# Output chains in halves, a corner turn moved, PSUM sums in W_down and a wider halo product, in a Hymba-style layer on one core

## The chip, the cores and the metric

The kernel runs on one NeuronCore of a Trainium2 chip. The metric is device time in microseconds (us), the median of several runs. TensorE is called PE, VectorE DVE, ScalarE ACT, GpSimd POOL and SyncE SP, as in the profile.

## The reference

One decoder layer, in float32, on 1024 tokens of width 1024 with 16 learned meta tokens in front:

```python
xn = rms_norm(h, mix_pre_g[l])
proj = xn @ w_in[l]                       # z, xbc, dt, q, k, v
y_ssd = ssd_mixer(z, xbc, dt_raw, ...)    # Mamba-2 scan in chunks of 128, gated and normed
y_sb = rms_norm(stick_breaking_attention(q, k, v).reshape(Bsz, L, SB_WIDTH), sb_norm_g[l])
mix = jnp.concatenate([y_ssd, y_sb], axis=-1) @ w_out[l]
h = h + rms_norm(mix, mix_post_g[l])
xn = rms_norm(h, ffn_pre_g[l])
gu = xn @ w_up[l]
g = causal_dwconv(gu[..., :D_FF], ffn_conv_w[l], ffn_conv_b[l])   # 3 taps
f = (jax.nn.gelu(g, approximate=True) * gu[..., D_FF:]) @ w_down[l]
h = h + rms_norm(f, ffn_post_g[l])
```

The attention has 16 heads of 64 and weighs key s for query t by beta[t,s] times the product of (1 - beta[t,j]) over the keys between them, so each block of 128 queries needs a running product along the keys. D_FF is 2816.

## The kernel before

All large products keep float32 accuracy with three float32r products: an operand is split into a high part (a rounding copy on ACT) and a low part (the difference, a subtraction), and high*high, low*high and high*low are summed in PSUM. So for each weight or activation tile there are an ACT copy and a subtraction on DVE or POOL ahead of TensorE. In the names, `yh`/`yl`, `whi`/`wlo`, `dh`/`dl` and `qh`/`ql` are such parts.

The kernel goes through these stages: norm and input projections with the SSD scan; stick-breaking attention over eight pairs of heads, with the projections of the next pair as filling work; the output projection in two halves of W_out (SSD half, attention half) with the residual and the second norm; W_up with the gate, as seven-product (Strassen-Winograd) blocks; W_down the same way. TensorE's order is the program's own from the attention on and again from the sixth row block of the second output half; there DVE, ACT and POOL are in program order too. In the attention and in the first five row blocks of the second output half a planner orders DVE, ACT, POOL and SP by its own costs.

**Attention, and the change's place in it.** For pair p and query block i, `block_weights` makes the scores `z` (L754) into PSUM pairs `zz` (two of them, shared with `tw`), ACT makes the two sigmoids `kp` and `bt` (L755, L756), DVE scans `kp` (L762), POOL multiplies `bt` by it (L764) and makes the edge columns `cb` (L765). `kp` has two buffers, `bt` three. `block_turn` transposes `bt` on TensorE (`tw`, L776) and ACT copies it out (`th`, L778). `block_mix` multiplies by the values (`av`, L791). Blocks run staggered: scores of block i, values of block i-3, filling work, the turn of block i-2. `turn_v` and `turn_edge` turn a pair's values into token order; `turn_edge` copies the edge columns (L419, L420), transposes them (`vtc`, L422), and prepares the meta tokens' queries, keys and values (`meta_q`, `meta_k`, a store to `mvd`). They are the `post` steps of a pair's projections, one per filling slot.

In the last pair the projections are used up, and the SSD half of the output projection fills in: `wout_steps` scales and splits eight tiles of W_out (`woa`, L876, L877), `split_y` splits the SSD output of a row block (L925 on ACT, L926 on POOL), and `ssd_half` runs for each of the eight row blocks two chains `out_steps` of 24 matmuls (`mo`, L936), one per 512 columns; ACT scales each into `ma` (L951) and SP stores it to `mixd`. One chain runs per query block, after the block's turn; three more while the last turns run out. `halo_rows` (L905) does the same product for the two last meta tokens in plain float32, on two output rows only, with the four column blocks of W_out in four groups of 32 array columns; ACT copies the four pieces out of PSUM into `mh` (L910, one buffer) and SP stores them to `halod` (L911). `halo_block` loads the two halves' rows again, scales and adds them on DVE (L1173, L1175), and passes them through the same residual and norm steps `after` as the other rows (L1097 to L1110; `oxn` is the normed row block that `turn_x2` transposes, L1116).

**W_down.** `DOWN` lists seven products, each of eleven steps of 256 rows. `split_step(s + 3)` splits the two operands of a later step (L1581, L1582; three buffers), `w_sum` makes sums of weight tiles on DVE (L1586; L1579 for product 6), `down_mm` runs 12 matmuls for four row blocks (L1652), each product in its own four PSUM banks. `todo` holds the evacuations of a finished product (`evac2`, into SBUF sums `facc`) and the tails, one item per step. The last 14 steps give the second low part to POOL. The last four steps run row block by row block, each followed by its sum (L1663), its square sum on ACT (L1687), the gain (L1688), POOL's power (L1697, L1698), and the closing multiply-add and store (`end_tail`, L1706).

Of the kernel before, what the change touches and what calls it, by code (L numbers as in the profile page):

```python
# [16 lines left out]
P = 128  # L17
# [34 lines left out]
def tile_layer(ctx: ExitStack, tc: tile.TileContext, x, meta, rows, parts,  # L52
# [80 lines left out]
    halod = [dr.tile([2, D], F32, name=f"halod{n}", tag=f"halod{n}") for n in range(2)]  # L133
# [227 lines left out]
    def qkv_steps(p, post):  # L361
# [67 lines left out]
        post += [lambda: turn_v(0), lambda: turn_v(1), turn_edge]  # L429
# [471 lines left out]
    def halo_rows(pool, half, y0, w, acc):  # L901
        for k in range(8):
            for s in range(2):
                for c in range(4):
                    mm(acc[32 * c:32 * c + 2, 0:256], y0[:, k, :], w[k][s][:, 256 * c:256 * c + 256].bitcast(F32),  # L905
                       start=k == 0 and s == 0, stop=k == 7 and s == 1)
        mh = pool.tile([P, 256], F32, tag="ma", name=f"mh{half}", bufs=1)
        for c in range(4):
            rows_ = slice(32 * c, 32 * c + 2)
            nc.scalar.activation(mh[rows_], acc[rows_, 0:256], AF.Copy)  # L910
            nc.sync.dma_start(out=halod[half][:, 256 * c:256 * c + 256], in_=mh[rows_])  # L911
# [7 lines left out]
    def split_y(pool, half, t, tags, yk=None):  # L919
# [6 lines left out]
        nc.gpsimd.tensor_tensor(yl, yk, yh.bitcast(F32), op=ALU.subtract)  # L926
        return yh, yl

    def out_steps(half, t, w, y, evac):
        yh, yl = y  # L930
        for hf in range(2):
            acc = psum_mm(f"mo{half}_{t}_{hf}")
            cs = slice(512 * hf, 512 * hf + 512)
            for k, (wh, wl) in enumerate(w):
                for j, (u, v) in enumerate(((yh, wh), (yl, wh), (yh, wl))):
                    mm(acc, u[:, k, :], v[:, cs], start=(k == 0 and j == 0), stop=(k == 7 and j == 2))  # L936
# [5 lines left out]
    def ssd_half(w, ys):  # L942
        for t in range(1, NT + 1):
            y = ys.pop(0)
            if t < NT - 1:
                ys.append(split_y(wp, 0, t + 2, ("whi", "wlo", WB)))

# [6 lines left out]
            yield from out_steps(0, t, w, y, ev)  # L954
# [19 lines left out]
    for p in range(8):  # L974
        for i in range(NT):
# [8 lines left out]
            run(fill, 1 + (i < FILL[p]))  # L984
            run(block)
# [16 lines left out]
            while len(ys1) < min(2, left[1]):  # L1002
                ys1.append(split_y(wp, 0, len(ys1) + 1, ("whi", "wlo", WB), yk[len(ys1)]))
# [18 lines left out]
    while turn or mix:  # L1022
# [4 lines left out]
        run(first, 1)  # L1027
    edge = edge_turn(7)
    run(first, 1)
# [27 lines left out]
    for _ in first:  # L1057
        run(second, 2)
# [785 lines left out]
```

## Time and profile before

| what | value |
|---|---|
| median of 3 runs | 1757.07 us (1756.71 to 1760.06) |
| the profiled execution | 1754.64 us, of which the span is 1752.8 us |
| mean granted TensorE clock | 0.994 of full speed |
| PE busy | 1711.4 us, 98% of the span |
| DVE, POOL, ACT busy | 1127.2, 890.3, 820.2 us |
| last pair's blocks and output chains | about 831 to 945 us of the span |
| second output half | about 983 to 1096 us |
| W_down | 1531 to 1745 us, the tail to 1752.8 us |

The span runs from the first to the last of the program's instructions. A row of an engine's timeline has the start, the time from there to the end, the engine, the line, the operation, what is written from what, the shapes, the count, and in brackets the engine's idle time before it and what ended it. Operations of one engine overlap at their ends, so what one costs in a row of them is the distance of the starts.

### The profile page before, as it was taken

How to read it: one execution, taken by the hardware profiler on the slowest of the kernel's cores; microseconds unless marked ns; L12 is line 12 of the kernel's file. 1: busy time of each engine (PE TensorE's matmuls, PEld its weight loads, DVE VectorE, ACT ScalarE, POOL GpSimd, SP SyncE). 2: the span in 40 equal slices, each digit the busy share in tenths (PEclk: the TensorE clock that was granted, in tenths of full speed). 3: DMA queues.
4: the chain of work that ended last, by engine and by line, in shares of the span. 5: the costliest groups of instructions: out<-in, count | busy, mean ns of one | idle time of the engine just before them, and what ended most of it. 6: DMA issues, size and time to landing. Idle time of an engine off the chain costs nothing. (4 is left out here: it accounts for less than half of the span.)

```text
span 1752.8 us, 28312 instructions
## 1 busy us (share of the span) xinstructions
PE 1711.4 (98%) x11358; PEld 1505.3 (86%) x11358; DVE 1127.2 (64%) x1225; ACT 820.2 (47%) x1363; POOL 890.3 (51%) x664
## 2 busy tenths in 40 slices
PE   7999999999999999999899989999999999999997
PEld 6999899788999998998678778889998888888885
DVE  5652964875676686668430457676666666757988
ACT  5423653554566566568453344533333333344453
POOL 4323663585566576556451233487776777400015
PEclk9999999999999999999999999999999999999999
DMA  4143343231011110112214543133332222395334
GB/s 161 50 116 93 107 128 105 65 103 38 26 37 37 38 35 27 37 60 74 81 49 145 199 156 132 62 119 98 106 106 91 90 91 90 122 331 185 96 121 162
DMA packets 90655, 173.87 MB, mean 99 GB/s; under 512 B 10694, under 2 KB 35798, under 8 KB 90524
## 3 DMA queue, kind: packets, MB, share of 16 engines
q1 hardware_dynamic: 90524, 172.07, 30.6%
q8 instruction: 89, 1.46, 0.3%
q14 instruction: 42, 0.34, 0.1%
HBM read 122.32 MB, written 49.72 MB: 98 GB/s over the span
## 5 line engine op out<-in xcount | busy, mean ns | idle before, releaser
L764 POOL TENSOR_TENSOR bt<-bt,kp 128x256 f32<-128x256 f32 (+7 forms) x128 | 212.7, 1681 | 180.4 <-DVE kp L762 150.7
L762 DVE TENSOR_TENSOR_SCAN kp<-kp,hold 128x272 f32<-128x272 f32 (+7 forms) x128 | 184.0, 1478 | 26.2 <-ACT kp L755 17.2
L1197 POOL TENSOR_TENSOR wlo<-wr,whi 128x1024 fp32r<-128x1024 f32 x43 | 107.5, 2508 | 38.0 <-ACT whi L1196 38.0
L1652 PE MATMUL dn<-dl,dh 128*128 128x512 f32 x304 | 118.7, 390 | 1.2 <-POOL dl L1582 1.2
L1652 PE MATMUL dn<-dh,dl 128*128 128x512 f32 x304 | 118.6, 390 | 0.1
L1652 PE MATMUL dn<-dh 128*128 128x512 f32 x304 | 118.5, 390 | 0.0
L1697 POOL TENSOR_TENSOR fms<-fms 128x1 f32<-128x1 f32 x8 | 5.6, 694 | 197.9 <-ACT dh L1581 185.8
L755 ACT ACTIVATE kp<-z 128x288 f32<-128x288 f32 (+6 forms) x112 | 82.6, 737 | 47.8 <-PE z L754 22.1
L1581 ACT ACTIVATE dh<-ar 128x512 fp32r<-128x512 f32 x76 | 48.1, 632 | 112.0 <-PE dn L1652 77.4
L1196 ACT ACTIVATE whi<-wr 128x1024 fp32r<-128x1024 f32 x43 | 45.6, 1060 | 114.8 <-PE fX L1254 68.3
L163 PE MATMUL pj_v<-xs,wh_v 128*128 128x400 f32 (+2 forms) x384 | 94.9, 334 | 0.0
L163 PE MATMUL pj_k<-xs,wh_k 128*128 128x400 f32 (+2 forms) x384 | 94.3, 332 | 0.0
L1326 DVE SCALAR_TENSOR_TENSOR ga<-gr,pp,ga 128x1024 f32<-128x1024 f32 x44 | 71.4, 1622 | 34.7 <-ACT ga L1319 33.9
L163 PE MATMUL pj_q<-xs,wh_q 128*128 128x386 f32 (+2 forms) x384 | 93.7, 331 | 0.0
L778 ACT ACTIVATE th<-tw 128x1024 f32<-128x1024 f32 (+2 forms) x96 | 75.7, 818 | 38.0 <-PE tw L776 37.8
L163 PE MATMUL pj_X<-xs,wh_X 128*128 128x400 f32 (+2 forms) x384 | 93.0, 329 | 0.0
L163 PE MATMUL pj_z<-xs,wh_z 128*128 128x386 f32 (+2 forms) x384 | 91.5, 326 | 0.0
L730 DVE CAST qh<-q 128x128 fp32r<-128x128 f32 x64 | 44.1, 690 | 63.9 <-PE z L754 63.6
L776 PE MATMUL tw<-ident,bt 128*128 128x128 f32 x576 | 78.1, 279 | 5.9 <-ACT bt L756 3.0
L1582 DVE TENSOR_TENSOR dl<-ar,dh 128x512 fp32r<-128x512 f32 x76 | 58.4, 768 | 39.1 <-ACT dh L1581 35.9
L756 ACT ACTIVATE bt<-z 128x288 f32<-128x288 f32 (+6 forms) x112 | 82.9, 740 | 0.0
L936 PE MATMUL mo<-woa,yh 128*128 128x512 f32 x256 | 82.4, 396 | 0.0
(556 smaller groups left out, 5532.3 us busy)
## 6 DMA issues: line engine op xcount, KB each, us to landing
wr<-in_w_up SPq DMA_DIRECT2D x44, 512.0 KB, 4.1
fds<-ga SPq DMA_DIRECT2D x44, 256.0 KB, 2.0
b<-in_w_down SPq DMA_DIRECT2D x44, 256.0 KB, 4.7
ar<-fds SPq DMA_DIRECT2D x44, 256.0 KB, 2.6
fda<-ga SPq DMA_DIRECT2D x33, 256.0 KB, 4.5
ar<-fda SPq DMA_DIRECT2D x33, 256.0 KB, 3.0
yk<-yd SPq DMA_DIRECT2D x16, 512.0 KB, 4.5
wor<-in_w_out SPq DMA_DIRECT2D x12, 512.0 KB, 3.9
```

The source lines that it names most:

```text
L163: mm(acc[:ncol, :n - s], a[:, k, :ncol], xs[c0][:, b, k, s:n], start=(k == 0 and j == 0), stop=(k == KB - 1 and j == 2))
L755: nc.scalar.activation(kp[:, :, a:a + w], z[:, :, :w], AF.Sigmoid, scale=-QSCALE)
L756: nc.scalar.activation(bt[:, :, a:a + w], z[:, :, :w], AF.Sigmoid, scale=QSCALE)
L762: nc.vector.tensor_tensor_scan(kp[:, j][:, ::-1], kp[:, j][:, ::-1], hold[:, L - n:L][:, ::-1], 0.0, op0=ALU.mult, op1=ALU.max)
L764: nc.gpsimd.tensor_tensor(bt[:, j, 0:m], bt[:, j, 0:m], kp[:, j, 1:m + 1], op=ALU.mult)
L776: nc.tensor.transpose(tw[:, j, b, :], bt[:, j, c0:c0 + P], ident)
L778: nc.scalar.activation(th[:, :, :nb, :], tw[:, :, :nb, :], AF.Copy)
L936: mm(acc, u[:, k, :], v[:, cs], start=(k == 0 and j == 0), stop=(k == 7 and j == 2))
L1197: nc.gpsimd.tensor_tensor(l, raw, h.bitcast(F32), op=ALU.subtract)
L1326: nc.vector.scalar_tensor_tensor(v, self.g[jj][:, :, i:i + 256], fconv_w[:, j, i:i + 1], v, op0=ALU.mult, op1=ALU.add)
L1582: (nc.gpsimd.tensor_tensor if k and s >= n2 - LATE else sub)(lo[k], raw, hi[k].bitcast(F32), op=ALU.subtract)
L1652: mm(banks[t], u[0][:, c], v[1], start=(p == 0 and i == 0), stop=(p == NPR - 1 and i == 2))
```

## The change

1. `out_steps` has a second stop in the middle of each chain, so `ssd_half` comes in 32 steps of 12 matmuls. In the last pair one step runs between a block's values and its turn, one after the turn; two at each place after the loop; the weights of the other half are spread one to each step. The split of the row block after next is issued in the middle of a row block's steps.
2. The low parts of the first two row blocks are made by DVE, and the second is split after the first half chain has been issued.
3. In the last pair `turn_edge` comes two filling slots later.
4. `halo_rows` multiplies each W_out part on its own: 512 columns at a time, high and low parts in separate groups, two rounds of evacuation, four rows of `halod` in place of two; `halo_block` loads and adds four.
5. W_down: products 1, 6, 7, 4 add up in one set of four banks, 2 and 5 start and 3 continues another; product 6 comes third. The evacuations are fewer, two of them at once after the product. All low parts are DVE's; the last three steps run row block by row block, with the tail reading PSUM.

```diff
-DOWN = [(1, "a11", "b11"), (2, "a12", "b21"), (3, "s4", "b22"), (6, "s2", "t2"), (5, "s1", "b11"), (7, "s3", "b12"),
+DOWN = [(1, "a11", "b11"), (2, "a12", "b21"), (6, "s2", "t2"), (5, "s1", "b11"), (3, "s4", "b22"), (7, "s3", "b12"),
         (4, "a22", "b21")]
+BANK = {1: "A", 2: "B", 6: "A", 5: "B", 3: "B", 7: "A", 4: "A"}
...
-        post += [lambda: turn_v(0), lambda: turn_v(1), turn_edge]
+        post += [lambda: turn_v(0), lambda: turn_v(1)] + [lambda: None] * (2 * (p == 7)) + [turn_edge]
...
     def halo_rows(pool, half, y0, w, acc):
         for k in range(8):
-            for s in range(2):
-                for c in range(4):
-                    mm(acc[32 * c:32 * c + 2, 0:256], y0[:, k, :], w[k][s][:, 256 * c:256 * c + 256].bitcast(F32),
-                       start=k == 0 and s == 0, stop=k == 7 and s == 1)
-        mh = pool.tile([P, 256], F32, tag="ma", name=f"mh{half}", bufs=1)
-        for c in range(4):
-            rows_ = slice(32 * c, 32 * c + 2)
-            nc.scalar.activation(mh[rows_], acc[rows_, 0:256], AF.Copy)
-            nc.sync.dma_start(out=halod[half][:, 256 * c:256 * c + 256], in_=mh[rows_])
+            for c in range(4):
+                mm(acc[32 * c:32 * c + 2, :], y0[:, k, :], w[k][c // 2][:, 512 * (c % 2):512 * (c % 2) + 512].bitcast(F32),
+                   start=k == 0, stop=k == 7)
+        for a in (0, 256):
+            mh = pool.tile([P, 256], F32, tag="ma", name=f"mh{half}_{a}", bufs=1)
+            for c in range(4):
+                b = 512 * (c % 2) + a
+                rows_ = slice(32 * c, 32 * c + 2)
+                nc.scalar.activation(mh[rows_], acc[rows_, a:a + 256], AF.Copy)
+                nc.sync.dma_start(out=halod[2 * half + c // 2][:, b:b + 256], in_=mh[rows_])
...
-        nc.gpsimd.tensor_tensor(yl, yk, yh.bitcast(F32), op=ALU.subtract)
+        eng.tensor_tensor(yl, yk, yh.bitcast(F32), op=ALU.subtract)
...
             for k, (wh, wl) in enumerate(w):
+                if k == 4:
+                    yield
...
-            yield from out_steps(0, t, w, y, ev)
+            for i, _ in enumerate(out_steps(0, t, w, y, ev)):
+                if i == 1 and t < NT - 1:
+                    ys.append(split_y(wp, 0, t + 2, ("whi", "wlo", WB)))
+                yield
...
             run(fill, 1 + (i < FILL[p]))
+            if first:
+                run(first, 1)
             run(block)
...
-            while len(ys1) < min(2, left[1]):
-                ys1.append(split_y(wp, 0, len(ys1) + 1, ("whi", "wlo", WB), yk[len(ys1)]))
+            if left[1] and not ys1:
+                ys1.append(split_y(wp, 0, 1, ("whi", "wlo", WB), yk[0], nc.vector))
...
                 run(first, 1)
+                ys1.append(split_y(wp, 0, 2, ("whi", "wlo", WB), yk[1], nc.vector))
...
-        run(first, 1)
+        run(first, 2)
     edge = edge_turn(7)
-    run(first, 1)
+    run(first, 2)
...
-    run(second, 2)
+    run(second, 1)
...
-        for n, r in enumerate((r_ssd, r_sb)):
+        for n, r in enumerate((r_ssd, r_ssd, r_sb, r_sb)):
...
-            (nc.gpsimd.tensor_tensor if k and s >= n2 - LATE else sub)(lo[k], raw, hi[k].bitcast(F32), op=ALU.subtract)
+            sub(lo[:, k], raw, hi[:, k].bitcast(F32), op=ALU.subtract)
...
-        for at, args in ((15 + 2 * k, ("b11", "b12", "b11", ALU.subtract)), (16 + 2 * k, ("b21", "b21", "b22", ALU.subtract)),
+        for at, args in ((18 + k, ("b11", "b12", "b11", ALU.subtract)), (16 + 2 * k, ("b21", "b21", "b22", ALU.subtract)),
...
     def evac2(n, t, acc):
         add = nc.vector.tensor_tensor
...
+        dst = facc[{1: (0, 0), 2: (0, 0), 6: (0, 1), 5: (1, 1), 3: (0, 1), 7: (1, 1)}[n] + (t,)]
+        if n in (1, 6, 5):
+            nc.scalar.activation(dst, acc, AF.Copy)
+        else:
+            add(dst, acc, dst, op=ALU.add)
...
-        f = facc[h, hf, t]
+        f = banks["A", t] if (h, hf) == (1, 0) else facc[h, hf, t]
...
-        if s > 2 and s < n2 - 4:
+        if s > 2 and s < n2 - 3:
             down_mm(s, (3, 0, 1, 2))
-        elif s == n2 - 4:
+            if p == NPR - 1 and n in (5, 7):
+                for t in (3, 0, 1, 2):
+                    evac2(n, t, banks[BANK[n], t])
+        elif s == n2 - 3:
...
-                for k in range(4):
+                for k in range(3):
                     down_mm(s + k, (t,))
-                evac2(n, t, banks[t])
                 half_tail(1, t, 0)
```

More of the change, by code (lines that the diff above doesn't have):

```diff
@@ L132, in tile_layer @@
     mixd = [dr.tile([P, D], F32, name=f"mixd{t}", tag=f"mixd{t}") for t in range(NT)]
-    halod = [dr.tile([2, D], F32, name=f"halod{n}", tag=f"halod{n}") for n in range(2)]
+    halod = [dr.tile([2, D], F32, name=f"halod{n}", tag=f"halod{n}") for n in range(4)]
     zd = [dr.tile([4, P, L], F32, name=f"zd{g}", tag=f"zd{g}") for g in range(2)]
@@ L1741, in tile_layer @@
             db = down.enter_context(tc.tile_pool(name="db", bufs=1, side="left"))
-            for h in range(2):
-                for hf in range(2):
-                    for t in range(4):
-                        facc[h, hf, t] = db.tile([P, 512], F32, tag=f"fa{h}{hf}{t}", name=f"facc{h}{hf}{t}")
+            for h, hf in ((0, 0), (0, 1), (1, 1)):
+                for t in range(4):
+                    facc[h, hf, t] = db.tile([P, 512], F32, tag=f"fa{h}{hf}{t}", name=f"facc{h}{hf}{t}")
             gfp = db.tile([P, D], F32, name="gfp", tag="gfp")
```

61 lines of the change are left out of this document (18 added, 43 removed).

## The prediction

> **What bounds the kernel now.** I read the page first, then the busy time by stretch, then the waits of TensorE, then the order of time on each engine around the longest of them.
>
> ```profile
> PE 1711.4 (98%) x11358; PEld 1505.3 (86%) x11358; DVE 1127.2 (64%) x1225; ACT 820.2 (47%) x1363; POOL 890.3 (51%) x664
> ```
>
> TensorE is busy 98% of a span of 1752.8 us. The change neither adds nor drops a 128-row matmul, so it can only move TensorE's idle time and its half-clock time. The busy time by stretch shows where those are (length, then busy us of PE, PEld, DVE, ACT, POOL, then the granted clock):
>
> ```profile
> core 0: us, PE busy (x) PEld busy (x) DVE busy (x) ACT busy (x) POOL busy (x), PEclk, DMA share, GB/s
> 833.90:842.80 8.90, 5.09 (x20) 4.12 (x21) 8.83 (x13) 1.74 (x3) 6.01 (x7) 0.62 0.30 80
> 860.00:890.60 30.60, 28.38 (x236) 21.45 (x229) 12.27 (x17) 15.12 (x28) 15.49 (x12) 1.00 0.21 71
> 890.60:898.00 7.40, 7.40 (x56) 6.01 (x55) 1.56 (x3) 4.47 (x7) 2.38 (x6) 0.77 0.10 37
> 898.00:912.00 14.00, 12.47 (x87) 9.95 (x86) 5.76 (x4) 8.34 (x13) 8.13 (x5) 1.00 0.17 57
> 1022.00:1031.00 9.00, 4.15 (x17) 3.39 (x16) 6.35 (x4) 2.27 (x5) 3.93 (x5) 0.81 0.39 117
> 1531.00:1745.00 214.00, 212.11 (x926) 172.97 (x924) 171.51 (x257) 98.70 (x186) 30.55 (x27) 1.00 0.54 180
> ```
>
> Rows 1 to 4 are the last attention pair. Idle there: 8.90 - 5.09 = 3.81 us, 30.60 - 28.38 = 2.22 us and 14.00 - 12.47 = 1.53 us. In the first row (1 - 0.62) x 8.90 = 3.4 us of clock is missing, which is 6.8 us at half; 1.84 us of that was idle anyway (the last two gaps in the next fence), so the clock cost (6.8 - 1.84)/2 = 2.5 us. In the third row (1 - 0.77) x 7.40 = 1.7 us is missing with TensorE never idle. Row 5 is the second output half, row 6 W_down, idle for 1.9 us in 214.
>
> ```profile
> 835.87 0.37 PE L422 MATMUL vtc<-ident,edge 128*128 128x128 f32 x1 [2.01 <-DVE edge L420]
> 837.70 1.11 PE L776 MATMUL tw<-ident,bt 128*128 128x128 f32 x4 [0.60 <-POOL bt L764]
> 840.05 1.97 PE L776 MATMUL tw<-ident,bt 128*128 128x128 f32 x8 [1.24 <-ACT bt L756]
> 817.51 2.39 DVE L731 TENSOR_TENSOR ql<-q,qh 128x128 fp32r<-128x128 f32 x1
> 827.20 6.70 DVE L762 TENSOR_TENSOR_SCAN kp<-kp,hold 128x1040 f32<-128x1040 f32 x2
> 838.94 0.29 DVE L731 TENSOR_TENSOR ql<-q,qh 128x128 fp32r<-128x128 f32 x1
> 817.36 2.40 POOL L926 TENSOR_TENSOR yl<-yk,yh 128x1024 fp32r<-128x1024 f32 x1
> 827.34 4.38 POOL L926 TENSOR_TENSOR yl<-yk,yh 128x1024 fp32r<-128x1024 f32 x1
> 831.69 5.96 POOL L764 TENSOR_TENSOR bt<-bt,kp 128x1024 f32<-128x1024 f32 x2
> 838.86 0.62 ACT L755 ACTIVATE kp<-z 128x544 f32<-128x544 f32 x1 [6.18 <-POOL cb L765]
> ```
>
> This is the order of time around the worst place, after the last query block of pair 6. Three TensorE waits follow one another: the corner turn waits for DVE's `edge`, the block's turn for POOL's `bt`, its second half for a PSUM bank that ACT empties late, because ACT itself waited 6.18 us for POOL's `cb`. All three hang on one DVE-POOL chain: scan, product, scan, product. In that chain stands POOL's `yl` at 827.34. The two engines lock each other out: `ql` takes 0.29 us alone and 2.39 us beside the first `yl`; the second `yl` pushes the product to 831.69.
>
> **Halves and moved steps in the last pair.** From block 2 on, an output chain of 24 matmuls runs after the block's turn `tw`; now 12 stand ahead of it and 12 behind.
>
> ```profile
> PE tw L776 <- ACT bt L756: 3.0, 4, 1.2
> PE z L754 <- ACT bt L756: 0.6, 1, 0.6
> 866.68 0.48 PE L936 MATMUL mo<-woa,yh 128*128 128x512 f32 x1
> 872.31 0.68 PE L829 MATMUL zm<-meta_k,meta_q 128*32 128x16 f32 x16
> ```
>
> A chain lasts 872.31 - 866.68 = 5.6 us, a half 2.8 us. The gaps of blocks 2 to 7 are at most 1.2 us each and nearly all ahead of `tw`, whose bank ACT has not yet emptied: 2.8 us of ready work covers each. In block 7 the third `z` and the second `tw` bank queue one behind the other on ACT, so 0.9 us stays there. The cost side: the next `z` now comes 2.8 us after `tw` where it came 5.6 us after, and needs a bank that `th`'s copies free. Of 2.22 + 1.53 = 3.75 us I take back 2.85 us; ends 1.0 and 3.75.
>
> At 833.9 four edits meet. The corner turn two slots later takes its 2.01 us wait off the path. It brings two `edge` copies, the transpose, ACT's copy, three small DVE operations and one store on SP, past one block turn and half a chain; the score matmuls at 872.31, 36 us after its old place, are the first to need its `meta_k`, so they are no worse off. The wait behind it remains: `tw` needs both products. The second `yl` moves to DVE and behind the first half chain, which frees POOL's stretch from 827.34, and the scans at 827.20 no longer wait for it. The first `yl` stays in its place and becomes a DVE operation. An equal-sized DVE subtraction with two SBUF inputs isn't in this stretch; the nearest are
>
> ```profile
> 1000.57 1.23 DVE L1101 TENSOR_TENSOR mb<-mb,xr 128x1024 f32<-128x1024 f32 x1
> 835.64 3.09 DVE L877 SCALAR_TENSOR_TENSOR woa<-wor,pp,woa 128x1024 fp32r<-128x1024 f32 x1
> ```
>
> 1.23 us with POOL quiet, 3.09 us beside POOL's product. I take 1.3 us, since POOL's own `yl` leaves an empty place there. DVE stood 2.1 us (2.39 - 0.29) behind that `yl`, so DVE gains 0.8 us or loses 1.0 us. So the scans come 0.8 us earlier and the second product some 3 us earlier (2.2 us for the absent second `yl`): ACT's copy of 838.86 comes near 835.9 and its pair of copies ends near 837.1, where `tw` resumed at 840.05. I expect TensorE to idle 2.1 us there in two pieces, under the 2.01 us in one piece that preceded the half clock, and the half clock not to come. Gain (3.81 - 2.1) + 2.5 = 4.2 us; ends 1.7 (clock still halved) and 6.3. The Trainium skill, page "TensorE: Matmul & The Clock Gate", section on HAM oscillation, puts the danger at idle gaps over about 3.4 us. By that no 2.01 us gap would halve the clock and its removal would give none of the 2.5 us back; here the clock was halved behind 2.01 us, and in the third row with no idle at all, so the measurement differs from the page. It is weighed below as a rival.
>
> The 1.7 us of the third row I leave where it is: the sixteen tiny matmuls ahead of it stay.
>
> **Halo in four groups.** Each group of 32 columns now makes 8 matmuls of 512 columns where it made 16 of 256, the same columns streamed.
>
> ```profile
> L905 PE MATMUL halo<-woa,y x128: 377/379/379, 856.3 to 863.0; 128*2 128x256 f32 x128
> 863.49 1.58 ACT L910 ACTIVATE mh<-halo 2x256 f32<-2x256 f32 x4 [5.41 <-PE halo L905]
> 984.80 0.22 SPq L1171 DMA_DIRECT2D mo<-halod  x1
> 982.18 1.42 SPq L911 DMA_DIRECT2D halod<-mh  x4
> ```
>
> 128 records in 6.7 us, each lasting 379 ns, so seven overlap; I price TensorE at 0 (ends -1 and +1). After it ACT makes two rounds of four copies, the second waiting until the first's four stores have landed (in the other half a load that reads them back issues at 984.80, 1.2 us after the last store's 983.60): 1.58 + 1.2 = 2.8 us more on ACT. ACT's `z` copies can stand behind, and `tw` behind those; TensorE has two short groups and half a chain, about 4.9 us, as cover. ACT's order isn't written by hand here. I take +0.4 us, ends 0 and 1.5. The second halo's extra loads and DVE operations have no reader near; see the rivals.
>
> **W_down.** Seven products of eleven steps; a step is 12 matmuls.
>
> ```profile
> 1597.35 0.69 DVE L1582 TENSOR_TENSOR dl<-ar,dh 128x512 fp32r<-128x512 f32 x1 [0.22 <-ACT dh L1581]
> 1597.96 0.68 DVE L1582 TENSOR_TENSOR dl<-b,dh 128x512 fp32r<-128x512 f32 x1
> 1600.07 0.69 DVE L1582 TENSOR_TENSOR dl<-ar,dh 128x512 fp32r<-128x512 f32 x1 [0.22 <-ACT dh L1581]
> L1581 ACT ACTIVATE dh<-ar 128x512 fp32r<-128x512 f32 x75 | 47.4, 632 | 109.6 <-PE dn L1652 77.4 <-issue 21.0 <-POOL dl L1582 4.9
> 1740.83 1.28 DVE L1706 SCALAR_TENSOR_TENSOR slotb22h<-slotb22h,fms 128x1024 f32<-128x1024 f32 x1
> PE dn L1652 <- POOL dl L1582: 1.2, 2, 0.6
> PE dn L1652 <- POOL d L1582: 0.6, 1, 0.6
> 1745.03 0.70 DVE facc L1663
> ```
>
> A step is 1600.07 - 1597.35 = 2.72 us, a DVE operation of 512 columns 1597.96 - 1597.35 = 0.61 us. Gains: the 1.8 us of waits for POOL, since no `lo` part is POOL's any more, and the last sum on DVE, 0.7 us after the last matmul, since the tail reads PSUM. Over the stage DVE loses 20 sums and takes 14 `lo` parts, but the timing shifts:
> - Product 6 comes third. In steps 18 to 28 meet two `lo` parts a step, b12 - b11 at every step, b21 - b22 at every other, the t2 sums of steps 19 to 29 and four evacuations of product 2. That is 53 operations, 32.3 us in 11 x 2.72 = 29.9 us; from step 20 on 45 in 9 steps, 27.5 us against 24.5 us, 3.0 us behind. The split runs about 3.5 us ahead (a `lo` pair is ready 0.63 + 1.2 us after a buffer comes free and is used 5.4 us after), less a hop through ACT for t2. Worked forward step by step, TensorE waits three or four times for 0.3 us: +1.1 us, ends 0 and 3.0.
> - Product 4 follows 7 in the same banks, so at step 66 TensorE waits for DVE's four sums. From the buffer's release: ACT copy 0.63, two `lo` 1.2, the closing multiply of block 2 1.28, sum 0.7, so bank 3 is free at 3.8 us, wanted at 2.72: +1.2 us; ends 0 and, with a second closing multiply still queued, 2.5. Product 3 behind 5 has ACT's copies in that place, which has room: 0.
> - In the last three steps DVE owes three `lo` parts that POOL had: +0.4 us, ends 0 and 1.
>
> Sum -1.8 - 0.7 + 1.1 + 1.2 + 0.4 = +0.2 us, ends -2.5 and +4.
>
> **Sum.** -2.85 - 4.2 + 0.4 + 0.2 = -6.45 us. The profiled execution took 1754.64 us (span 1752.8 us and 1.84 us around it), so 1748.2 us; it lies 2.43 us under the median of the three runs, 1757.07 us, so I forecast 1750.6 us. A difference under 0.2%, 3.5 us, can't be told from none.
>
> **Rivals.** (1) The half clock comes anyway. For it: the third row has it without idle time, so a gap is not what it needs. Against: the second row keeps 1.00 with 2.22 us idle in short pieces. Then 2.5 us stay: 1753.1 us. The Trainium skill's page named above would have it go this way.
>
> (2) The pair isn't refilled: ACT, DVE and POOL are not ordered by hand in it, DVE is 8.83 us busy of 8.90 there, and the first `yl` at 3.09 us instead of 1.3 delays both scans; half chains then meet `z` waiting for `th`. Both pair terms shrink to about 1 us and the W_down ends rule: 1757 us, at most 1760.
>
> (3) Slower: the second halo's chain stands in front of DVE's `oxn`.
>
> ```profile
> 1022.35 3.87 DVE L1110 SCALAR_TENSOR_TENSOR mo<-mb,rs_ff,gffn 2x1024 f32<-2x1024 f32 x1 [1.80 <-POOL rs_ff L190]
> 1027.56 0.66 PE L1116 MATMUL x2tp<-ident,oxn 128*128 128x128 f32 x2 [4.85 <-DVE oxn L1110]
> DMA to landing us min/median/max: 4.4/4.4/4.4
> 989.93 1.26 DVE L1175 SCALAR_TENSOR_TENSOR mb<-mo,r_sb,mb 2x1024 f32<-2x1024 f32 x1
> ```
>
> It already costs 4.85 us. Two more groups mean two more rounds through one tile: load (4.4 us at most), operation 1.26 us, on SP and DVE in turn, 11.3 us. Its sum is ready at 989.93 + 1.26 = 991.2 and the operation in front of `oxn` comes 31 us later, so it decides only if the order leaves less than 11 us between them; then TensorE waits up to 11 us more, 1761 us. If the shift moves the chain out of `oxn`'s way instead, up to 6.5 us come back (4.85 and the clock of row 5): 1744 us.
>
> **How the numbers follow.** Forecast 0.50, its own range 1746 to 1754 us; rival 1 0.14; rival 2 0.17; rival 3 0.12; its mirror 0.07. Faster by over 0.2% is the forecast but for a twentieth, the mirror and a third of rival 1: 0.59. Slower is most of rival 3 and a quarter of rival 2: 0.14. Same: 0.27. The range takes in the forecast, rivals 1 and 2 up to 1758.5 us, and part of the mirror: 1744.5 to 1758.5 us.
>
> **What would show it.** Right: `vtc` waits for nothing; TensorE's idle time between blocks 1 and 7 of pair 7 falls from 7.6 us to about 3; the clock at 834 to 843 reads 1.00; W_down shows no wait for POOL, one of about 1.2 us at the first step of product 4, small ones near step 30. Wrong: `tw` waiting for ACT after the first half chain, `z` for `th`, a gap over 5 us at `oxn`, or DVE waits of over 3 us in W_down.

## The result, and the profile after

The kernel after takes 1756.46 us (median of 19 runs, 1752.23 to 1756.84), the kernel before beside it 1757.6 us (19 runs, 1755.1 to 1760.19). The ratio is 0.9984, 95% interval 0.9978 to 0.9990: 2.8 us less, between 1.8 and 3.9. The two medians are only 1.1 us apart and the two means 2.4 us, so the size of the gain is known to a microsecond or two, not better. The forecast was 1750.6 us with 1744.5 to 1758.5 us as its range, so the time lies in the range, but 5.9 us over the forecast and outside the forecast's own part of the range, 1746 to 1754 us. By the forecast's own bound of 0.2% that is no difference.

The profiled execution took 1756.31 us (span 1754.2 us), at the median, where that of before lay 2.43 us under its own. First the page's busy line, then the busy time in the same stretches of time as before (columns as there).

```profile
PE 1714.0 (98%) x11230; PEld 1503.6 (86%) x11230; DVE 1119.9 (64%) x1223; ACT 825.1 (47%) x1375; POOL 862.5 (49%) x648
```

```profile
core 0: us, PE busy (x) PEld busy (x) DVE busy (x) ACT busy (x) POOL busy (x), PEclk, DMA share, GB/s
833.90:842.80 8.90, 5.88 (x57) 4.85 (x55) 8.83 (x11) 2.94 (x5) 6.76 (x6) 0.90 0.21 60
860.00:890.60 30.60, 29.73 (x211) 22.13 (x200) 13.90 (x17) 18.31 (x34) 16.89 (x13) 1.00 0.18 61
890.60:898.00 7.40, 7.40 (x46) 5.94 (x46) 3.73 (x4) 3.79 (x6) 3.75 (x6) 0.77 0.24 74
898.00:912.00 14.00, 12.69 (x90) 10.10 (x89) 3.06 (x2) 9.14 (x14) 6.50 (x4) 1.00 0.10 37
1022.00:1031.00 9.00, 3.06 (x15) 2.55 (x14) 5.86 (x4) 2.77 (x5) 3.81 (x5) 0.69 0.31 78
1531.00:1745.00 214.00, 212.16 (x927) 172.99 (x926) 157.11 (x253) 101.22 (x190) 7.47 (x12) 1.00 0.55 180
```

The 128 matmul records fewer than before are the two halo products, 64 each instead of 128. Idle time in the second and fourth stretch fell from 3.75 to 2.18 us. In W_down POOL's work fell from 30.55 to 7.47 us and DVE's from 171.51 to 157.11 us, and TensorE is idle as long as before. The stall in the second output half (row 5) has grown.

The stretches of time don't hold quite the same work: both programs run the same TensorE instructions up to the `av` of the last block but one of pair 6 (28 matmuls), yet after reaches it at 835.13 us and before at 832.12 us, because the half clock fell at 57.7 us before, and at 325.6 and 424.6 us after. (In a run below with one piece of half clock ahead of it, at 57.6 us, the `av` comes at 832.14 us.) So I compare from that `av`, between instructions that both kernels have:

```
                                             before    after
start of that av to end of pair 6's last tw    9.91     7.91
start of that av to second halo product      142.51   140.04
second halo product to first W_down matmul   556.57   557.60
first W_down matmul to end of the last one   213.80   213.89
end of the last matmul to end of the span      7.81     7.55
```

By stretch the change gave 2.47 us in the pair, lost 1.03 us in the second output half, lost 0.09 us in W_down and gave 0.26 us in the tail: 1.6 us of the 6.45 that were forecast.

These are differences between one execution of each kernel, and like code takes a microsecond more or less in the other profiles. From the end of pair 6's last `tw` to the second halo product it took 132.6 us before and 132.1 us after. Three runs below whose output chains are those of before (the corner turn alone, W_down alone, and the last, four `yl` by DVE alone) took 133.7 to 133.8 us there, and two with those of after (both `yl` on POOL, W_down's sums spread) 131.5 and 131.2 us. The half clock near 890 us, in the profiles of both kernels, is in none of these five. From the second halo product to W_down the corner turn alone and W_down alone took 557.4 and 557.6 us, with the code of before and 6.8 us of half clock where before has 3.4; four runs with the code of after took 557.9 to 558.7 us. So the pair's gain may be larger than 2.47 us, and the 1.03 us lost behind it is no better known.

At the entry, the order of time on the four engines is now (four rows of TensorE, then DVE, POOL, ACT; the bracket is the idle time ahead and what ended it):

```profile
835.13 1.75 PE L792 MATMUL av<-th,v 128*64 128x128 f32 x28
836.81 0.66 PE L777 MATMUL tw<-ident,bt 128*128 128x128 f32 x4
838.72 0.66 PE L777 MATMUL tw<-ident,bt 128*128 128x128 f32 x4 [1.25 <-POOL bt L765]
841.07 1.97 PE L777 MATMUL tw<-ident,bt 128*128 128x128 f32 x8 [1.69 <-ACT bt L757]
820.13 1.26 DVE L928 TENSOR_TENSOR yl<-yk,yh 128x1024 fp32r<-128x1024 f32 x1
825.68 2.73 DVE L928 TENSOR_TENSOR yl<-yk,yh 128x1024 fp32r<-128x1024 f32 x1
830.38 4.54 DVE L763 TENSOR_TENSOR_SCAN kp<-kp,hold 128x1040 f32<-128x1040 f32 x2
832.87 5.79 POOL L765 TENSOR_TENSOR bt<-bt,kp 128x1024 f32<-128x1024 f32 x2 [2.62 <-ACT bt L757]
839.88 0.62 ACT L756 ACTIVATE kp<-z 128x544 f32<-128x544 f32 x1 [4.18 <-POOL cb L766]
```

`vtc` no longer waits, the scans take 4.54 us where they took 6.70, and ACT waits 4.18 us where it waited 6.18. But the second `yl` is not behind the first half chain: DVE, which the planner orders here, makes it at 825.68, beside POOL's product and ahead of the scans. The waits of TensorE in the last pair (us in total, times, longest):

```profile
PE tw L777 <- ACT bt L757: 3.5, 3, 1.7
PE tw L777 <- POOL bt L765: 1.3, 1, 1.3
PE mo L940 <- ACT mh L912: 0.9, 1, 0.9
```

The third is new: a half chain waits for the PSUM bank that ACT's second round of halo copies empties. Later there are two more waits, one in the second output half that has grown (4.85 us before) and a new one in W_down:

```profile
PE x2tp L1123 <- DVE oxn L1117: 5.9, 1, 5.9
1715.94 0.47 PE L1654 MATMUL dnA<-dh 128*128 128x512 f32 x1 [1.75 <-DVE facc L1663]
```

### The profile page after: what moved, and what is told of

Its sections match the earlier page's. It is cut to its first block, busy times and chain, and to the rows that moved or that the text cites. A ratio compares the mean times of both kernels' runs of the same rounds, so it can differ in the third digit from the quotient of the medians.

```text
span 1754.2 us, 28052 instructions
## 1 busy us (share of the span) xinstructions
PE 1714.0 (98%) x11230; PEld 1503.6 (86%) x11230; DVE 1119.9 (64%) x1223; ACT 825.1 (47%) x1375; POOL 862.5 (49%) x648
## 5 line engine op out<-in xcount | busy, mean ns | idle before, releaser
L1584 DVE TENSOR_TENSOR dl<-ar,dh 128x512 fp32r<-128x512 f32 x77 | 53.2, 691 | 51.0 <-ACT dh L1583 51.0
L792 PE MATMUL av<-th,v 128*64 128x128 f32 x1152 | 78.4, 281 | 0.0
L777 PEld LDWEIGHTS tw<-ident,bt 128*128 128x128 f32 x576 | 66.1, 142 | 10.4 <-ACT bt L757 4.2
L792 PEld LDWEIGHTS av<-th,v 128*64 128x64 f32 x1152 | 62.4, 138 | 13.9 <-issue 11.3
```

Of the source, the lines that this page charges most:

```text
L777: nc.tensor.transpose(tw[:, j, b, :], bt[:, j, c0:c0 + P], ident)
L792: mm(av[halves[j], :], v[:, kb, halves[j]], th[:, j, b, :], start=kb == 0, stop=kb == i)
```

## The experiments

The `av` that the expectations call that of block 4 is the one above. "Entry" is the time from its start to the end of pair 6's last `tw`.

**The corner turn two slots later, on the kernel before.**

```diff
-        post += [lambda: turn_v(0), lambda: turn_v(1), turn_edge]
+        post += [lambda: turn_v(0), lambda: turn_v(1)] + [lambda: None] * (2 * (p == 7)) + [turn_edge]
```

> The kernel before with one edit: the last pair's corner turn two filling slots later. Theory A (its 2.01 us wait ran beside the wait of the block turn for the same chain of scans and products): the corner turn no longer waits, the block turn behind it waits 1.8 us more ahead of its first transposes, TensorE resumes the second half of the block turn at the same 8 us after the last score matmuls of that block, and the total stays within 1 us of the kernel before. Rival B (the forecast's reading, that the wait is given back): TensorE is about 2 us earlier at the first output chain and the total 2 us or more under the kernel before, with the half clock gone.

1759.26 us, ratio 1.0004 (0.9994 to 1.0014). TensorE's order of time:

```profile
833.50 1.75 PE L791 MATMUL av<-th,v 128*64 128x128 f32 x28
837.09 0.66 PE L776 MATMUL tw<-ident,bt 128*128 128x128 f32 x4 [1.84 <-POOL bt L764]
839.05 0.66 PE L776 MATMUL tw<-ident,bt 128*128 128x128 f32 x4 [1.30 <-POOL bt L764]
841.40 1.97 PE L776 MATMUL tw<-ident,bt 128*128 128x128 f32 x8 [1.69 <-ACT bt L756]
```

The wait at `vtc` is gone, and `tw` waits 1.84 us in its place. Entry is 9.87 us, as before. The forecast's 2.01 us for this part was no gain: POOL's product is as late as `edge`.

**Output chains in halves, on the kernel before.**

```diff
             for k, (wh, wl) in enumerate(w):
+                if k == 4:
+                    yield
...
             run(fill, 1 + (i < FILL[p]))
+            if first:
+                run(first, 1)
             run(block)
...
```

The steps of the other places are doubled to match.

> The kernel before with one edit: output chains in halves, half a chain ahead of each block turn of the last pair, and the steps of the other places doubled to match. Theory A (half a chain covers the waits, but each cut of a chain costs TensorE about 0.1 us and the waits were partly covered already): idle time from block 2 to block 7 falls from 3.75 us to about 1.3 us, from the first output chain to the second halo TensorE is 1 to 2 us faster, and the total 1 to 2 us under the kernel before. Rival B (the forecast): 2.85 us faster over that stretch. Rival C (scores now wait for the block turn's copies, as they come half a chain after it): new waits of z, nothing gained.

1757.38 us, ratio 0.9996 (0.9986 to 1.0006). Idle time in the pair's blocks 2 to 7 fell from 3.75 to 1.31 us, so the 12 matmuls do cover `tw`. It was handed back at the end of the half, in a wait for an output bank (row of TensorE's waits, then ACT's order of time):

```profile
PE mo L938 <- ACT ma L953: 2.0, 1, 2.0
962.38 3.21 ACT L876 ACTIVATE wohb<-worb,pp 128x1024 fp32r<-128x1024 f32 x3
965.50 1.25 ACT L953 ACTIVATE ma<-mo,r_ssd 128x512 f32<-128x512 f32 x2
```

ACT has three high parts of the second half's weights in front of the evacuation `ma`; none of the three readings above had this wait. In the kernel after this wait isn't there; from the first output matmul to the second halo product after took 132.48 us, before 132.95 us.

**Both `yl` back on POOL, the rest of after kept.**

```diff
-                ys1.append(split_y(wp, 0, 1, ("whi", "wlo", WB), yk[0], nc.vector))
+                ys1.append(split_y(wp, 0, 1, ("whi", "wlo", WB), yk[0]))
```

and the same for the second.

> The kernel after, with both `yl` subtractions back on POOL, at the new places; nothing else changes. Same measure, start of `av` of block 4 to the end of the last turn of pair 6: 9.90 before, 9.67 with the halves alone, 9.87 with the later corner turn alone, 7.91 after. Theory A (the 2.0 us gained there is the work of the engine change, since the other two parts alone gave 0.2 and 0.0): 9.5 to 9.9 us, the first `ql` again over 2 us long beside POOL's `yl`, and total 1758.5, 2 over after. Rival B (the halves and the later corner turn give it together, each one alone being covered by the other's wait): 7.7 to 8.3 us and total within 1 us of after, 1756.5.

1758.06 us, ratio 0.9993 (0.9984 to 1.0002); entry 9.91 us. DVE and POOL stand again as before:

```profile
821.54 2.40 DVE L732 TENSOR_TENSOR ql<-q,qh 128x128 fp32r<-128x128 f32 x1
831.23 6.70 DVE L763 TENSOR_TENSOR_SCAN kp<-kp,hold 128x1040 f32<-128x1040 f32 x2
831.37 4.38 POOL L928 TENSOR_TENSOR yl<-yk,yh 128x1024 fp32r<-128x1024 f32 x1
835.71 5.96 POOL L765 TENSOR_TENSOR bt<-bt,kp 128x1024 f32<-128x1024 f32 x2
```

Without the engine change nothing of the 2.0 us at the entry is left: Theory A holds. The engine change without the other parts was not run.

**The second `yl` really late.** In the kernel after, y2's raw tile is loaded where it is split, not ahead.

```diff
-                      load_y(0, 2, rp.tile([P, L], F32R, tag="rk", name="yk0_2", bufs=3).bitcast(F32)[:, :D]
-                             .rearrange("p (a b) -> p a b", b=P))]
...
-                ys1.append(split_y(wp, 0, 2, ("whi", "wlo", WB), yk[1], nc.vector))
+                ys1.append(split_y(wp, 0, 2, ("whi", "wlo", WB), None, nc.vector))
```

> The changed kernel with the second row block's raw tile loaded only where that block is split, so that neither ACT's copy nor DVE's low part of it can be ordered ahead of the last scans of pair 6. Theory A (the expected gain at the last query block of pair 6 was lost because DVE, ordered by the planner, makes both low parts ahead of the last scans, 1.26 and 2.73 us): the last scans start some 2.5 us earlier against the first score matmuls of block 1 of pair 7, POOL's edge product with them, and TensorE's two waits of 1.25 and 1.69 us there shrink to about 1 us in all; with so little idle time the half clock there stays away, and the total is 2 to 4 us under the changed kernel's. Rival B (the chain of scans and products is as long as it is, whatever stands ahead): the two waits stay at 2.5 us or more and the total within 1 us.

1758.2 us, ratio 0.9999 (0.9988 to 1.001). The scans now come ahead of the second `yl`; entry fell to 5.88 us, and the gain was lost at the next block (two rows of DVE's order of time, one of TensorE's waits, two of ACT's order of time):

```profile
829.11 4.57 DVE L763 TENSOR_TENSOR_SCAN kp<-kp,hold 128x1040 f32<-128x1040 f32 x2
842.90 1.59 DVE L928 TENSOR_TENSOR yl<-yk,yh 128x1024 fp32r<-128x1024 f32 x1
PE z L755 <- ACT th L779: 4.0, 1, 4.0
845.71 1.06 ACT L927 ACTIVATE yh<-yk 128x1024 fp32r<-128x1024 f32 x1 [2.71 <-DMA yk<-yd]
846.67 1.92 ACT L779 ACTIVATE th<-tw 128x1024 f32<-128x1024 f32 x2
```

y2 now sits in the buffer that y3's load needs. That load is issued late, ACT stands 2.71 us for it, and `th`'s copies, which free the bank for `z`, are queued behind. The half clock, 3.4 us of it, comes behind that wait, at 847.7 us. Theory A is right about the order and wrong about the total.

**The same, with y3 loaded early** into y1's raw tile:

```diff
-                    ys.append(split_y(wp, 0, t + 2, ("whi", "wlo", WB)))
+                    ys.append(split_y(wp, 0, t + 2, ("whi", "wlo", WB), load_y(0, 3, yk[0]) if t == 1 else None))
```

> The kernel after, with the second row block's raw tile loaded only where it is split (as in the run that did that alone) and the third's raw tile loaded early, into the tile that the first has left. Measured from the start of the values of block 4 (`av`, 28 matmuls) to the end of the last turn of pair 6: before 9.90, after 7.91, with the late second split 5.89 us; from the same start to the second halo product 142.5 before, 140.0 after. Theory A (the forecast's step was right in size, 4.2 us, and what lost 2.0 of it is DVE's second `yl` ahead of the scans; with the late split the gain was handed back because the third tile's load had no buffer and ACT stood 2.7 us for it, in front of `th`): entry 5.9 us, the 4.05 us wait of `z` for `th` goes to under 0.6, stretch to the second halo 138.0 us, total 1754.5 (2 under after's 1756.5). Rival B (any split of two tiles in that stretch delays `th` on ACT, whichever load comes first): entry 5.9, but `z` waits 2 us or more for `th` and the stretch stays at 139.5 to 140.5, total 1756 to 1758.

1754.29 us, ratio 0.9974 (0.9963 to 0.9984). Entry 5.94 us, `av` to second halo 137.12 us, in an execution of 1751.61 us, the fastest of seven. ACT's order of time, and the wait that is left:

```profile
841.01 1.05 ACT L927 ACTIVATE yh<-yk 128x1024 fp32r<-128x1024 f32 x1
841.96 1.93 ACT L779 ACTIVATE th<-tw 128x1024 f32<-128x1024 f32 x2
PE z L755 <- ACT th L779: 1.2, 1, 1.2
```

The rows of the two runs show both causes: the order of `yl` and the scans at the entry, and the load without a buffer, which handed the gain back in the run above. `z` still waits 1.2 us, twice what Theory A allowed. The stretch's time does not size them: this profile lacks the half clock that after has at 841.1 and 892.3 us, 3.4 us each, worth up to 1.7 us apiece. By the ratios the gain over after is some 1.8 us (0.9984 - 0.9974), and their intervals overlap, so it is not shown in the time.

**The halo product in two groups, the rest of after kept.** `halo_rows`, `halod` and the load loop are those of before. "Two groups" and "four groups", here and below, count the tensors of `halod` that `halo_block` loads and adds; on TensorE both products use four groups of 32 columns.

> The changed kernel with the halo product of before: 16 matmuls of 256 columns in each group, four copies and four stores, two rows to load and add. Theory A (the second round of copies holds a PSUM bank and the longer chain of loads and sums delays the normed row block): the 0.87 us wait of the output chain for the halo's copy goes, the wait for oxn falls from 5.94 to about 4.85 us, the halo's own stretch on TensorE stays at 7.05 us, and the total falls by about 2 us. Rival B (both waits come from the place in the order, not from the four groups): the wait for oxn stays at 5.9 us, and the total moves by under 1 us. Rival C (wider matmuls are cheaper on TensorE): the halo's stretch grows by over 0.3 us.

1753.24 us, ratio 0.9966 (0.9954 to 0.9978). A halo product takes 7.09 us on TensorE, with four groups 7.05 us. The waits:

```profile
PE x2tp L1122 <- DVE oxn L1116: 5.7, 2, 5.5
PE z L755 <- ACT th L779: 0.6, 1, 0.6
```

The wait for `mh` is gone, `oxn` waits 5.45 us at its longest instead of 5.94 (4.85 before, which Theory A expected back), and `av` to second halo takes 138.14 us. Of those 1.9 us, 0.77 lie at the entry, ahead of the halo: the half clock that fell at 841.1 us in after isn't there in this profile. By the ratios the four groups cost some 3.2 us (0.9984 - 0.9966; the intervals meet at 0.9978), of which the trace accounts for the 0.87 us at `mh` and the 0.5 us at `oxn`. The rest is open: the profiled execution, 1751.10 us, is the fastest of its eight.

**W_down alone, on the kernel before.** `DOWN`, `BANK` and all of W_down as in after.

> The kernel before with W_down alone as changed, its sums where the change put them. Theory A (the part is worth nothing by itself: the waits for GpSimd and the last sum go, and DVE's own queue gives as much back): first to last W_down matmul 213.8 us (213.89 before), a wait of 1.7 us for DVE's sum at the first step of product 4, the tail behind the last matmul 7.5 us (7.81 before), total within 1 us of before. Rival B (after the changed pair the stage starts in another place of the clock's windows, and alone it gains what the forecast gave it without DVE's queue): stretch 211.5 us, total 2 us or more under before.

(That text, the next one and that of the three edits together exchange two numbers: 213.80 us is before and 213.89 after.) 1757.94 us, ratio 0.9998 (0.9989 to 1.0007); W_down 213.89 us, the wait at product 4 1.8 us, the tail 7.69 us. Theory A holds: the part is worth nothing by itself.

**W_down's sums spread, on the kernel after.**

```diff
-                         (16 + 2 * k, ("b21", "b21", "b22", ALU.subtract)),
+                         (29 + k, ("b21", "b21", "b22", ALU.subtract)),
...
-        if todo:
+        if todo and s not in (63, 64):
             todo.pop(0)()
```

> The kernel after, with W_down's eleven sums b21 - b22 at steps 29 to 39, one a step, instead of every other step from 16, and no evacuation or tail step taken at steps 63 and 64, so that DVE has none queued at the turn from product 7 to product 4. Theory A (W_down's two new waits are DVE's queue, 1.4 us near 1600 to 1640 and 1.75 us at the first step of product 4): both waits under 0.3 us, W_down from first to last matmul 213.80 to 210.8 us, total 1753.5. Rival B (DVE has 157 us of work in 214, so the order of its sums decides little; the matmuls lose their time elsewhere, or the wait for the four sums at the turn between products stays, since the banks are shared): stretch 213 to 214 us, the wait at product 4 over 1 us, total within 1 us of after.

1752.73 us, ratio 0.9964 (0.9952 to 0.9976). W_down took 210.46 us; its busy time by stretch:

```profile
1532.60:1743.20 210.60, 210.47 (x926) 173.15 (x924) 157.30 (x253) 101.30 (x190) 8.44 (x14) 1.00 0.55 181
```

TensorE waits nowhere in it, with as much work on DVE as in after (157.1 us). What the change had removed and what DVE's queue gave back were each some 3.4 us (213.89 - 210.46).

**The halo's residual and norm one row block earlier**, on the run with two halo groups.

```diff
-        if t == 2:
+        if t == 1:
             turn_halo = halo_block()
```

> The kernel after, with the halo product of before (two groups, as in the run that did that alone: 1753.24 us) and the halo's residual and norm put behind the first row block of the second output half instead of the second. Theory A (TensorE's wait for the second `oxn`, 5.45 us there, 5.94 after, 4.85 before, is the halo's last operation of 3.87 us standing in front of it on DVE; the first `oxn` has 4.5 us of room, 1006.8 to 1011.3, and the halo's sum is ready near 992): no wait over 0.5 us at either, the half clock at 1023 to 1027 gone (another 1.7 us), total 1753.2 - 5.45 - 1.7 = 1746. Rival B (the chain only moves in front of the first `oxn`, whose room it uses up: its norm goes through POOL twice and the 3.87 us operation comes last): a wait of 3 to 6 us at the first `x2tp`, the half clock behind it, total 1752 to 1754.

1752.82 us, ratio 0.9965 (0.9953 to 0.9977), as without it. DVE's order of time and the row of TensorE's waits:

```profile
1007.68 3.87 DVE L1116 SCALAR_TENSOR_TENSOR mo<-mb,rs_ff,gffn 2x1024 f32<-2x1024 f32 x1 [1.85 <-POOL rs_ff L191]
1011.48 1.27 DVE L1116 SCALAR_TENSOR_TENSOR oxn<-mb,rs_ff,gffn 128x1024 f32<-128x1024 f32 x1
PE x2tp L1122 <- DVE oxn L1116: 4.5, 2, 4.3
```

Rival B: the chain stands in front of the first `oxn` instead. In this profile `tw` waited 2.81 us already at 819 us, so its entry (4.36 us) is not comparable.

**Three edits together**: late y2 with early y3, two halo groups, spread sums.

> The kernel after with three of the runs' edits together: the late second split with the third tile loaded early, the halo product of before, and the spread sums in W_down. Theory A (they lie in different stretches and add): start of `av` of block 4 to second halo 140.04 to 137.12 by the first, 0.87 less by the second, W_down 213.80 to 210.46 by the third, the `oxn` wait 5.94 to 5.45 by the second: 1756.5 - 2.9 - 0.9 - 3.3 - 0.5 = 1749 us. Rival B (a stall that goes lets the next one show, as with the late split alone, where `z` waited 4.05 us in its place): `z` <- `th` or the `oxn` wait grows by 1 to 3 us and the total is 1751 to 1752.

1750.17 us, ratio 0.9950 (0.9937 to 0.9962), by the ratios some 6 us under after. W_down 210.46 us, no `mh` wait, `oxn` 5.5 us: those two add. `av` to second halo is 137.21 us, as with the y tiles alone, so the halo's 0.9 us does not show there; this profile has 3.4 us of half clock at 888 us, the other none.

**Four `yl` of the second output half by DVE**, on the run before.

```diff
-            ys.append(split_y(op, 1, t + 1, ("yh", "yl", 2)))
+            ys.append(split_y(op, 1, t + 1, ("yh", "yl", 2), None, nc.vector if t < 6 else nc.gpsimd))
```

> The run before it in this call with one edit more: in the second output half the low parts of y's row blocks 3 to 6 by VectorE instead of GpSimd. Theory A (the halo's last operation lasts 3.87 us because POOL's `yl` of 2.33 us, 1024.40 to 1026.73, locks DVE out for that long; the same kind of operation lasts 1.27 us elsewhere): the operation takes 1.3 us, the second `oxn` comes 2.6 us earlier, its wait falls from about 5.5 to about 3 us, the four `yl` of 1.2 to 1.3 us each find DVE idle: 1749 - 2.6 = 1746.4, less if the half clock behind the wait goes too. Rival B (3.87 us is the operation's own, as it was the same in five kernels, or the new DVE operations take the place that is gained): the operation stays at 3.9 us or the wait at 5 to 6 us, total within 1 us of the other run.

1742.68 us, ratio 0.9913 (0.9900 to 0.9927). The order of time in the run without this edit, POOL's rows and then DVE's:

```profile
1004.65 2.39 POOL L927 TENSOR_TENSOR yl<-yk,yh 128x1024 fp32r<-128x1024 f32 x1 [4.32 <-ACT yh L926]
1007.13 0.22 POOL L190 TENSOR_SCALAR ms_mo<-oss 128x1 f32<-128x1 f32 x1
1019.84 2.33 POOL L927 TENSOR_TENSOR yl<-yk,yh 128x1024 fp32r<-128x1024 f32 x1
1008.04 1.28 DVE L1104 SCALAR_TENSOR_TENSOR mb<-mb,rs_mo,gpost 128x1024 f32<-128x1024 f32 x1 [5.42 <-POOL rs_mo L191]
1019.38 3.87 DVE L1114 SCALAR_TENSOR_TENSOR mo<-mb,rs_ff,gffn 2x1024 f32<-2x1024 f32 x1 [1.80 <-POOL rs_ff L191]
1023.17 1.27 DVE L1114 SCALAR_TENSOR_TENSOR oxn<-mb,rs_ff,gffn 128x1024 f32<-128x1024 f32 x1
```

and DVE and TensorE's wait with the four moved:

```profile
1004.99 1.28 DVE L1104 SCALAR_TENSOR_TENSOR mb<-mb,rs_mo,gpost 128x1024 f32<-128x1024 f32 x1 [0.77 <-POOL rs_mo L191]
1016.33 1.27 DVE L1114 SCALAR_TENSOR_TENSOR mo<-mb,rs_ff,gffn 2x1024 f32<-2x1024 f32 x1 [1.80 <-POOL rs_ff L191]
1017.53 1.27 DVE L1114 SCALAR_TENSOR_TENSOR oxn<-mb,rs_ff,gffn 128x1024 f32<-128x1024 f32 x1
PE x2tp L1120 <- DVE oxn L1114: 1.5, 1, 1.5
```

The operation takes 1.27 us instead of 3.87, as Theory A has it. A second effect was not expected: at 1004.65 POOL's `yl` also stood in front of the second row block's norm, which now comes 3.05 us earlier (1008.04 and 1004.99; the second halo product starts at 971.0 us in both). Not all of that is POOL's: ACT's copy ahead of the norm's square sum starts 1.6 us earlier too, at 1001.89 and not 1003.52 us. Together the second `oxn` comes 5.6 us earlier. TensorE no longer waits for it (the 1.5 us are at a later row block, at 1087.5 us), and the half clock behind it is gone too. This is the fastest kernel here, by the ratios some 12.5 us under after.

**The same edit alone, on the kernel before.**

> The kernel before with that one edit alone: in the second output half the low parts of y's row blocks 3 to 6 by VectorE; nothing of the change is in it. From the second halo product to the first W_down matmul: 556.6 us before, 557.6 after, 557.4 in the kernel with three edits, 551.6 with this fourth. Theory A (the stall at `oxn` and the half clock behind it are GpSimd's `yl`, ahead of the second row block's norm and beside the halo's last operation, and were there before the change): stretch 550.5 to 552 us, the `oxn` wait under 1.5 us, the halo's last operation 1.3 us, total 1751.5, 6 to 7 under before. Rival B (the early halo product of two groups and the shorter pair are needed for it, since only then the halo's sum is ready in time): stretch over 554 us, `oxn` waits over 2.5 us, total 1755 or more.

1751.72 us, ratio 0.9961 (0.9947 to 0.9975).

```profile
1022.50 1.27 DVE L1110 SCALAR_TENSOR_TENSOR mo<-mb,rs_ff,gffn 2x1024 f32<-2x1024 f32 x1 [1.79 <-POOL rs_ff L190]
PE x2tp L1116 <- DVE oxn L1110: 1.5, 1, 1.5
```

Second halo to first W_down matmul took 551.5 us instead of 556.6. So this stall is not of the change's making, and the one line is worth more than the whole change: 0.9961 against 0.9984, with intervals that do not meet.

## Why the prediction was right or wrong

The sign and the range held, the size did not: 6.45 us were forecast, the ratio gives 2.8 us and the stretches of the two profiles 1.6 us. Of the 4.85 us between forecast and stretches 4.2 are in the pair, 1.0 in the second output half; W_down and the tail gave 0.4 more than forecast. The range held because it took in rivals 1 and 2. Of the signs named for right and wrong, `vtc` waits for nothing and W_down waits for no POOL operation; the idle time fell from 7.6 only to 5.2 us (3.02 + 2.18) and the clock at the entry reads 0.90. Two of the signs for wrong came: the gap at `oxn` is over 5 us, and `tw` waits 1.3 us for ACT behind a half chain, at 910 us.

- **The entry, forecast 4.2 us, measured 2.0.** Two steps failed. "The second `yl` moves to DVE and behind the first half chain" took a place in the program for a place in time; the planner put it at 825.68, ahead of the scans. With the data late enough to force that order, the entry shrank by 4.0 us (9.91 to 5.88) with no half clock in it, so the step's size was right under its condition. And the 2.01 us of `vtc` were counted as taken off the path, though the text said that "the wait behind it remains": the wait of `tw` for POOL's product filled that time. The first `yl` was priced at 1.3 us and took 1.26.
- **The half clock there, forecast gone.** It came at 841.1 us for 3.4 us, half as long as before: neither the forecast, which has it gone, nor rival 1, which has it whole. With the same edits at the entry it is missing in the run with two halo groups. In the six profiles with both `yl` on POOL it lasted 6.8 us there each time; what decides is open.
- **Blocks 2 to 7, forecast 2.85 us, measured 0.47** between the two kernels' profiles, 2.3 to 2.6 us between the other five named with the stretches. The halves took idle time from 3.75 to 1.31 us, 2.44 us, near the forecast. Then 0.87 us of ACT's halo copies came in. The cut chains themselves cost TensorE something that I had at nothing: at the full clock a half takes 2.86 to 2.96 us from start to start, half a chain 2.82 us (5.63/2), over twelve halves an estimated 1.1 us. By how much the place of the half clock shifts the measured number is open.
- **The halo, forecast +0.4 us.** TensorE's price of 0 was right (7.09 and 7.05 us); ACT's rounds cost 0.87 us, within the ends of 0 and 1.5.
- **Rival 3, at a tenth of its price.** `oxn`'s wait grew from 4.85 to 5.94 us, not by 11 us. Its reading of the cause was incomplete: the row of 3.87 us was in the prediction, but not that POOL's `yl` beside it makes up 2.6 of it.
- **W_down, forecast +0.2 us, measured -0.17.** The step at product 4 measured 1.75 us (forecast 1.2), the last steps wait 0.07 (0.4), the waits for POOL are gone, and undoing the two pile-ups gives 3.4 us, against 2.3 us that the forecast gave them together. From first matmul to first matmul a product takes 29.92 us, in after the third one 31.65 us: 1.7 us for the pile-up that was forecast at 1.1. The last product fell from 34.27 to 30.72 us, by 3.5 us, where the waits for POOL had been put at 1.8, and the tail gave 0.26 us instead of 0.7. So that the sum came out within 0.4 us was luck: terms that were off by 0.4 to 2 us cancelled.

Of the rivals the second was nearest, though not as told: the idle time of blocks 2 to 7 was filled, and DVE's order at the entry kept half of the gain there.

## What to carry to other kernels

Where a planner orders an engine, a new place in the program moves an operation only if its data or its buffer keep it there; find the operation in the trace of a like case, or tie it to a load, and then look at what that load's buffer delays. A wait that ends no later than the next one in line is worth nothing, however long it is. And before costing an edit, look for an operation that lasts three times as long as its like: here one of 3.87 us beside those of 1.27 us led to the largest gain, outside the change.

## What the runs showed of the hardware

A DVE operation lasts longer beside POOL's `yl` at three places: `ql` 0.29 or 2.40 us, the two scans 4.54 or 6.70 us, the halo's last operation 1.27 or 3.87 us. The Trainium skill, page "SBUF — State Buffer", section on who interferes with whom, says that a DVE instruction with two SBUF inputs contends with a GpSimd instruction that reads SBUF, and calls the shared port an exclusive lock; the first and third case agree.

Ahead of the tail the half clock comes in pieces of 3.41 or 6.83 us in all fourteen profiles, and lands in different places from run to run of like code: at 836.0 us for 6.8 us before, at 841.1 us for 3.4 us after, and not at all around there with two halo groups, though `tw` waits 1.3 and 1.7 us in both of the last two. In the wait for `oxn` of 4.3 to 6.3 us in twelve profiles it came each time, beginning 2.0 to 5.2 us into the wait, and in the two where that wait is gone it did not. The Trainium skill, page "TensorE: Matmul & The Clock Gate", section on HAM oscillation, puts the danger at idle gaps over about 3.4 us; the gaps at `oxn` are longer than that, though the half clock begins as early as 2.0 us into one; the piece near 890 us with TensorE never idle (7.40 us busy of 7.40) does not agree, and what starts that one stays open.
